# Float32 products of the compression as three float32r products, and a 0/1 operand loaded one chunk earlier

## The chip, the cores and the metric

The kernel runs on one core of a Trainium2 chip. The metric is the device time of one execution in microseconds (us); lower is better. Times of the kernel before are three executions and one profiled execution.

## The reference, cut to what matters

One inference step of a decoder trunk with two layers, for a prompt of 512 positions and eight samples of 8 positions with a past of 1024. Each layer projects its input into columns for a convolution, for sparse attention with three branches and for differential attention. One of the three branches attends to compressed keys and values, and the change lies in this compression:

```python
def nsa_compress(k, pe, w1, b1, w2):
    B, L, G, D = k.shape
    n16 = L // CMP_STRIDE
    k16 = k[:, :n16 * CMP_STRIDE].reshape(B, n16, CMP_STRIDE, G, D)
    blk = jnp.concatenate([k16[:, :-1], k16[:, 1:]], axis=2) + pe[None, None, :, None, :]
    blk = blk.transpose(0, 1, 3, 2, 4).reshape(B, n16 - 1, G, CMP_LEN * D)
    return jax.nn.gelu(blk @ w1 + b1) @ w2
```

CMP_STRIDE is 16, CMP_LEN 32, G 2 and D 64: each block of 32 positions (2048 numbers of a group) is multiplied by w1 (2048 x 128), once for keys and once for values, in both layers. The past of the samples lies in pages that a page table names. The samples' three branches are mixed by sigmoid gates, `o = gate0 * o_cmp + gate1 * o_sel + gate2 * o_win`.

## The kernel before, in words

Each layer first runs two streams of work side by side: `projections()` (the input projection in column chunks b, the convolution's columns, then d, c, q, e, with the convolution's 62 taps on VectorE beside them) and `compressions()` (keys, then values). Both are Python generators that yield the estimated cost of what they have just issued; `merge` always continues the stream that is behind by its share, WP and WC. The tile framework then orders each engine's instructions by a simulated timeline of its own, so an engine's order need not be the program's.

Working tiles come from two sets of SBUF slots: U, 30 slots of 1152 words a partition, and H, 26 slots of 512. `W` takes the slot that has been free longest, and the first write into it waits until the last user is done. `load` issues on SP's queue, in order. `gather` issues an indirect DMA from GpSimd (POOL).

`compress` works in five chunks: four with two samples each (N = 256 columns of output: 2 samples, 2 groups, 64 blocks) and one with the prompt (N = 64). `cmp_keys` gathers a sample's past as 128 partitions (a stretch of 8 positions each, 128 numbers a position), transposes it on TensorE in pieces of 128x128 (L757, eight a tile), and copies each pair out of PSUM with `cp` (L217, nearly always ScalarE), 64 partitions at a time, eight copies a tile. The result kt holds key columns by stretch; a small tail of four columns carries the position term pe, which the first chunk turns into the bias. Then 16 products (L227, as all products) of a float32 piece of w1 by every second column of kt add up in one PSUM bank:

```python
mm(hid[:, :N + 1], w1[k], kt[jp // 2][:, jp % 2, aa:aa + 2 * N + 1:2], k == 0, k == 15)
```

In a trace a float32 product stands as two MATMUL records with a weight load each; a float32r product stands as one. The rest of the kernel's large products are made of float32r parts already: `split` rounds a number to float32r on ScalarE (L187) and subtracts that on VectorE (L190), and three products, high by high, high by low and low by high, take the place of one.

`sample_queries` runs before chunk e. Its first step spreads the samples' gates over partitions by four small products with `selp`, a 0/1 matrix of 64 x 512 that it loads itself from the constants; then it transposes the samples' queries (L1068), which VectorE has scaled at L667.

Of the kernel before, what the change touches and what calls it, by code (L numbers as in the profile page):

```python
# [45 lines left out]
YA = 1.0  # L46
RATIO2 = 3
WP = 125.0
WC = 120.0
WPR = 145.0  # L50
WS = 150.0
ALPHA = (2 * DEPTH) ** 0.25
# [83 lines left out]
def kernel(ctx: ExitStack, tc: tile.TileContext, a: dict, o: dict, nlayers: int = DEPTH):  # L136
# [33 lines left out]
    def T(tag, shape, dt=F):  # L170
        return sb.tile(shape, dt, tag=tag, name=f"{tag}_{next(uid)}", bufs=1)
# [5 lines left out]
    def PS(tag, dt=F):  # L177
        return ps.tile([128, 512], dt, tag=tag, name=f"{tag}_{next(uid)}", bufs=PBUFS[tag])

    def load(out, in_):  # L180
        nc.sync.dma_start(out, in_)
# [31 lines left out]
    def cp(out, in_):  # L213

        if next(turn) % ratio[0] == 1:
            return V.tensor_copy(out, in_)  # L216
        return S.activation(out, in_, AF.Copy)  # L217
# [237 lines left out]
    def layer(l, x, x_src, raws):  # L455
# [165 lines left out]
        def new_kv(br):  # L621
            vv[br] = W("H", [128, 4, 128])
            kH[br], kL[br] = (W("U", [128, 2, SEQ], FR) for _ in range(2))
# [66 lines left out]
        def attention_columns():  # L690
            for c in ORDER:
                if c == "c":
                    new_kv("win")
                if c == "e":
                    sample_queries()
                    yield 2.0
                    own["QK"] = yield from diff_operands(0, "t1")
                yield from chunk(*dict(d=(1816, 512, sink_d), e=(2328, 256, sink_e), c=(1536, 280, sink_c), q=(512, 512, sink_q))[c])
            free(*x[0], *x[1], *x[2])
# [18 lines left out]
        G.memset(vblk, 0.0)  # L718

        def cmp_weights(which):  # L720
            w1s = [W("U", [128, 8, 128]) for _ in range(2)]
            for i in range(2):
                load(w1s[i], a["cmp_w1_" + which][l, i * 1024:(i + 1) * 1024].rearrange("(k p) n -> p k n", p=128))
            w1 = [w1s[k // 8][:, k % 8] for k in range(16)]
            w2p = T("c2", [128, 192])
            G.memset(w2p, 0.0)
            load(w2p[:, 0:64], a["cmp_w2_" + which][l])
            load(w2p[:, 128:192], a["cmp_w2_" + which][l])
            pe = W("H", [16, 128])
            load(pe, a["cmp_pe_" + which][l].rearrange("(k r) d -> k (r d)", r=2))  # L730
            b1 = T("cb" + which, [128, 1])
            load(b1, a["cmp_b1_" + which][l].unsqueeze(1))
            pt = PS("t1")
            PE.transpose(pt[:, :16], pe, ident[:16, :16])
            peT = T("cpe" + which, [128, 2, 2, 4])
            V.tensor_copy(peT, pt[:, :16].rearrange("p (a q i) -> p q i a", q=2, i=2))
            free(pe)
            return w1s, w1, w2p, b1, peT

        def cmp_keys(which, peT, p):  # L740


            n = 128 if p < 4 else 64
            slots = 4 if p < 4 else 2
            kt = [W("U", [128, 2, slots * n + 4]) for _ in range(2)]
            for q in range(2):
                V.tensor_copy(kt[q][:, :, slots * n:], peT[:, q])
            for b2 in range(2 if p < 4 else 1):
                if p < 4:
                    nat = gather("cache_nsa_cmp_" + which, l, 2 * p + b2)  # L750
                else:
                    nat = W("U", [64, 8, 128])
                    load(nat, o["p_cmp_" + which][l, 0].rearrange("(p j) g d -> p j (g d)", j=8))
                for q in range(2):
                    pt = PS("t1").rearrange("p (k t) -> p k t", k=4)
                    for j in range(4):
                        PE.transpose(pt[:, j, :n], nat[:, 4 * q + j], ident[:n, :n])  # L757
                    for g in range(2):
                        c0 = (b2 * 2 + g) * n
                        for par in range(2):  # L760
                            cp(kt[q][par * 64:(par + 1) * 64, :, c0:c0 + n], pt[g * 64:(g + 1) * 64, par::2, :n])
                    yield 0.5
                free(nat)
            return kt

        def cmp_out(which, w2p, p, N, xb):
# [27 lines left out]
        def compress(which):  # L794
            w1s, w1, w2p, bias, peT = cmp_weights(which)
            yield 6.0
            held = None
            for p in range(5):
                kt = yield from cmp_keys(which, peT, p)
                N = 256 if p < 4 else 64  # L800
                hid = PS("h")
                for k in range(16):
                    aa, jp = k // 4, k % 4
                    mm(hid[:, :N + 1], w1[k], kt[jp // 2][:, jp % 2, aa:aa + 2 * N + 1:2], k == 0, k == 15)
                    if k % 4 == 3:
                        yield 1.8
                free(*kt)
                if p == 0:
                    add(bias, hid[:, N:N + 1], bias)
                xb = W("H", [128, N])  # L810
                act(xb, hid[:, :N], AF.Identity, bias=bias)
                t1 = W("H", [128, N])
                act(t1, xb, AF.Square, scale=math.sqrt(0.044715 * GELU_C))
                V.scalar_tensor_tensor(out=t1, in0=t1, scalar=GELU_C, in1=xb, op0=OP.add, op1=OP.mult)
                act(t1, t1, AF.Tanh)
                V.scalar_tensor_tensor(out=xb, in0=t1, scalar=1.0, in1=xb, op0=OP.add, op1=OP.mult)
                free(t1)
                if held:
                    cmp_out(which, w2p, *held)
                held = (p, N, xb)  # L820
                yield 1.5
            cmp_out(which, w2p, *held)
            free(*w1s)

        def compressions():
            yield from compress("k")
# [219 lines left out]
        def sample_queries():  # L1046
            nonlocal QSR, QDs, QS, QR, QD
            QSR, QDs = W("U", [128, 2, 4, 128]), W("U", [128, 2, 4, 128])
            QS, QR = QSR[:, 0], QSR[:, 1]
            QD = [QDs[:, 0], QDs[:, 1]]  # L1050
            qr_s, za_s, zr_s = own["qr"], own["za"], own["zr"]
            pg = PS("t1")
            selp = W("H", [64, 512])
            so = CST["selp"][0]
            load(selp, a["cst"][:64, so:so + 512])
            for p in range(4):
                mm(pg[:, p * 24:(p + 1) * 24], selp[:, p * 128:(p + 1) * 128], gates[:64, 4], True, True)
            free(selp)
            gm = T("gm", [128, 4, 3, 8])
            for p in range(4):  # L1060
                mul(gm[:, p], pg[:, p * 24:(p + 1) * 24].rearrange("p (h r) -> p r h", r=3), C("headm").unsqueeze(1).to_broadcast([128, 3, 8]))
            V.tensor_reduce(grow.rearrange("p a b -> p (a b)"), gm.rearrange("p a b h -> p (a b) h"), axis=AX.X, op=OP.add)
            G.memset(QS, 0.0)
            G.memset(QR, 0.0)
            for src, dst in ((qr_s.rearrange("p (h d) -> p h d", h=4), QS), (za_s.rearrange("p h g d -> p h (g d)"), QR)):
                pt = PS("t1")
                for k in range(4):
                    PE.transpose(pt[:, k * 64:(k + 1) * 64], src[:, k], ident[:64, :64])  # L1068
                for b2 in range(2):
                    for g in range(2):  # L1070
                        gr = slice(g * 64, (g + 1) * 64)
                        c0 = b2 * 64 + g * 32
                        cp(dst[gr, :, c0:c0 + 32].rearrange("p q (k t) -> p q k t", k=4),
                           pt[gr, :256].rearrange("p (k q b t) -> p q b k t", k=4, q=4, b=2)[:, :, b2])
            pt = PS("t1")
            V.tensor_scalar(zr_s[:, :256], zr_s[:, :256], DSCALE, None, op0=OP.mult)
            for k in range(4):
                PE.transpose(pt[:, k * 64:(k + 1) * 64], zr_s[:, k * 128:(k + 1) * 128], ident[:64, :64])
            dm = C("dmask").rearrange("p (f k) -> p f k", f=2)
            for ft in range(2):  # L1080
                for b2 in range(2):
                    src = pt[:, ft * 64:(ft + 1) * 64].rearrange("p (q b t) -> p q b t", q=4, b=2)[:, :, b2]
                    mul(QD[ft][:, :, b2 * 64:(b2 + 1) * 64].rearrange("p q (k t) -> p q k t", k=8), src.unsqueeze(2).to_broadcast([128, 4, 8, 8]),
                        dm[:, ft].unsqueeze(1).unsqueeze(3).to_broadcast([128, 4, 8, 8]))
            cp(ktd.rearrange("p f t -> p (f t)"), pt[:, 128:256])
            free(qr_s, za_s, zr_s)
# [548 lines left out]
```

## Time and profile before

| | |
|---|---|
| median of three executions | 2062.5 us (2058.97 to 2068.48) |
| the profiled execution | 2071.4 us, of which its span (first to last instruction) is 2069.6 |
| TensorE products busy | 1933.5 us (93%), 12222 records |
| TensorE weight loads busy | 1631.7 us (79%) |
| VectorE busy | 1101.2 us (53%) |
| ScalarE busy | 916.7 us (44%) |
| POOL busy | 206.7 us (10%) |
| mean granted TensorE clock | 0.969 of full speed |

All times in the trace are us from the span's start. Busy time of TensorE's products counts each from its start to the modelled end of its drain, so products that follow each other closely overlap, and the pace is read from one start to the next, not from the mean duration. DVE is VectorE, ACT ScalarE, PE TensorE, SP the queue that most loads go through.

### The profile page before, as it was taken

The numbers are of one execution on the slowest core, as the hardware profiler recorded it, in microseconds if no ns is written. First come the engines' busy times: TensorE is split into PE (matmuls) and PEld (weight loads), VectorE is DVE, ScalarE is ACT, GpSimd is POOL, SyncE is SP. The second block draws the span as 40 slices with busy tenths as digits, with TensorE's granted clock in tenths as the row PEclk, the third lists the DMA queues.
The fourth block names the chain that finished last, engine by engine and source line by source line (L and its number), as shares of the span: only waits on it lengthen the run. The fifth ranks groups of instructions, "written<-read, shape, count | busy, mean of one in ns | idle before, by whom it ended". The sixth has DMA issues, their size and how long they took to land. (4 is left out here: it accounts for less than half of the span.)

```text
span 2069.6 us, 32882 instructions
## 1 busy us (share of the span) xinstructions
PE 1933.5 (93%) x12222; PEld 1631.7 (79%) x12222; DVE 1101.2 (53%) x3012; ACT 916.7 (44%) x2368; POOL 206.7 (10%) x233
## 2 busy tenths in 40 slices
PE   8999888989999999999999997989899999999997
PEld 6887765656689999988879776656566899999885
DVE  3568476866573333323456665678666633333236
ACT  3635565767422333321245545667673223333211
POOL 2011022121010000000120110221110000000002
PEclk9999899999999999999999998999999999999999
DMA  6423143243423332352153321441433332324411
GB/s 200 137 76 103 28 145 128 83 146 99 136 92 117 97 122 83 93 187 77 48 174 108 96 71 45 152 155 57 138 108 118 112 122 82 122 84 130 149 56 51
DMA packets 190252, 223.91 MB, mean 108 GB/s; under 512 B 19092, under 2 KB 138812, under 8 KB 189948
## 3 DMA queue, kind: packets, MB, share of 16 engines
q1 hardware_dynamic: 171660, 154.69, 24.5%
q0 software_dynamic: 18432, 67.12, 10.2%
q8 instruction: 97, 1.59, 0.3%
q14 instruction: 63, 0.52, 0.1%
HBM read 206.23 MB, written 24.15 MB: 111 GB/s over the span
## 5 line engine op out<-in xcount | busy, mean ns | idle before, releaser
L227 PE MATMUL a<-H,U 128*128 128x512 f32 (+3 forms) x2264 | 552.8, 411 | 14.0 <-ACT H L187 11.6
L190 DVE TENSOR_TENSOR H<-H,H 128x512 fp32r<-128x512 f32 (+5 forms) x392 | 255.5, 657 | 510.5 <-ACT H L187 482.8
L227 PEld LDWEIGHTS a<-H,U 128*128 128x128 f32 (+1 forms) x2264 | 386.2, 190 | 111.2 <-issue 15.4
L187 ACT ACTIVATE H<-H 128x512 fp32r<-128x512 f32 (+4 forms) x418 | 240.8, 583 | 519.9 <-DMA H<-in_ffn_w_dram 298.8
L227 PE MATMUL a<-U,H 128*128 128x288 f32 (+2 forms) x3008 | 399.2, 306 | 7.9 <-DMA U<-in_cache_diff_v_dram,idx 6.7
L227 PEld LDWEIGHTS a<-U,H 128*128 128x128 f32 (+1 forms) x3008 | 370.2, 181 | 21.7 <-DMA U<-in_cache_diff_v_dram,idx 7.3
L227 PE MATMUL t<-U,H 128*128 128x288 f32 x1584 | 288.7, 297 | 0.4 <-ACT U L187 0.4
L227 PEld LDWEIGHTS t<-U,H 128*128 128x128 f32 x1584 | 243.5, 190 | 1.0 <-ACT U L187 0.6
L227 PE MATMUL a<-U,U 128*128 128x512 f32 (+4 forms) x744 | 200.7, 379 | 7.9 <-ACT H L187 3.7
L227 PE MATMUL h<-U,U 128*128 128x257 f32 (+5 forms) x708 | 152.4, 376 | 13.1 <-ACT U L217 13.0
L217 ACT ACTIVATE U<-t 64x256 f32<-64x256 f32 (+4 forms) x393 | 142.8, 366 | 45.6 <-PE t L757 24.5
L227 PEld LDWEIGHTS a<-U,U 128*128 128x128 f32 x744 | 129.4, 191 | 34.2 <-ACT U L187 7.4
L227 PEld LDWEIGHTS h<-U,U 128*128 128x128 f32 (+1 forms) x708 | 114.6, 185 | 40.3 <-ACT U L217 17.3
L227 PE MATMUL h<-U,H 128*128 128x288 f32 x528 | 140.9, 296 | 0.0
L187 ACT ACTIVATE U<-H 128x288 fp32r<-128x288 f32 (+4 forms) x160 | 64.4, 438 | 143.8 <-DVE H L190 104.1
L217 ACT ACTIVATE H<-t 128x512 f32<-128x512 f32 (+1 forms) x172 | 94.9, 564 | 45.6 <-PE t L1145 23.5
L547 DVE SCALAR_TENSOR_TENSOR U<-U,cw,U 128x512 f32<-128x512 f32 x240 | 109.4, 510 | 0.1
L227 PEld LDWEIGHTS h<-U,H 128*128 128x128 f32 x528 | 99.3, 188 | 0.0
L190 POOL TENSOR_TENSOR U<-U,U 128x512 f32<-128x512 f32 x24 | 33.6, 1417 | 599.1 <-DVE rs_u L321 459.9
L187 ACT ACTIVATE U<-t 128x256 fp32r<-128x256 f32 (+4 forms) x132 | 47.1, 370 | 97.0 <-PE t L350 40.8
L190 DVE TENSOR_TENSOR U<-H,U 128x64 fp32r<-128x64 f32 (+6 forms) x204 | 69.9, 385 | 31.1 <-ACT U L187 24.8
L216 DVE COPY H<-t 128x512 f32<-128x512 f32 (+1 forms) x92 | 57.2, 626 | 45.7 <-PE t L1214 15.6
(293 smaller groups left out, 2268.9 us busy)
## 6 DMA issues: line engine op xcount, KB each, us to landing
H<-in_ffn_w_dram SPq DMA_DIRECT2D x264, 256.0 KB
H<-in_w_in_dram SPq DMA_DIRECT2D x64, 256.0 KB
H<-in_w_out_dram SPq DMA_DIRECT2D x32, 256.0 KB
xd<-U SPq DMA_DIRECT2D x24, 256.0 KB
U<-xd SPq DMA_DIRECT2D x12, 512.0 KB
U<-in_x_prompt_dram SPq DMA_DIRECT2D x8, 512.0 KB
H<-in_state_nsa_win_v_dram SPq DMA_DIRECT2D x16, 256.0 KB
H<-in_state_nsa_win_k_dram SPq DMA_DIRECT2D x16, 256.0 KB
```

The costliest lines, as they stand in the source:

```text
L187: S.activation(out, in_, func, **kw)
L190: return (eng or V).tensor_tensor(out, x, y, op=op)
L216: return V.tensor_copy(out, in_)
L217: return S.activation(out, in_, AF.Copy)
L227: return PE.matmul(out, lhsT, rhs, start=start, stop=stop)
L547: V.scalar_tensor_tensor(out=ac, in0=ex, scalar=wc, in1=ac, op0=OP.mult, op1=OP.add)
```

## The change

The gathered tile is first copied inside SBUF by ScalarE, four copies a tile, into two halves (H slots) whose columns are ordered so that each 128 of them, transposed, are already two positions of one group. The halves are transposed, four pieces each, and `split` into two float32r tiles kt (high and low). w1 is loaded into a passing tile and split into high and low parts, four tiles that are held instead of two. The products of a chunk run in two halves (q), each with its own kt; each float32 product becomes three float32r products. The tail of pe has six columns in two parts, copied by GpSimd instead of VectorE. The cost yields change from 1.8 per four products to 1.4 per twelve, and WC from 120 to 128. `selp` is loaded before chunk q, into an H slot that it holds through that chunk, instead of in `sample_queries`.

```diff
-WC = 120.0
+WC = 128.0
@@ attention_columns
+                if c == "q":
+                    own["selp"] = W("H", [64, 512])
+                    load(own["selp"], a["cst"][:64, CST["selp"][0]:CST["selp"][0] + 512])
@@ cmp_weights
-            w1s = [W("U", [128, 8, 128]) for _ in range(2)]
+            w1s = [[], []]
             for i in range(2):
-                load(w1s[i], a["cmp_w1_" + which][l, i * 1024:(i + 1) * 1024].rearrange("(k p) n -> p k n", p=128))
-            w1 = [w1s[k // 8][:, k % 8] for k in range(16)]
+                raw = W("U", [128, 8, 128])
+                load(raw, a["cmp_w1_" + which][l, i * 1024:(i + 1) * 1024].rearrange("(k p) n -> p k n", p=128))
+                wh, wl = (W("U", [128, 8, 128], FR) for _ in range(2))
+                split(wh, wl, raw)
+                free(raw)
+                w1s[0].append(wh)
+                w1s[1].append(wl)
+            w1 = [(w1s[0][k // 8][:, k % 8], w1s[1][k // 8][:, k % 8]) for k in range(16)]
...
-            peT = T("cpe" + which, [128, 2, 2, 4])
-            V.tensor_copy(peT, pt[:, :16].rearrange("p (a q i) -> p q i a", q=2, i=2))
+            peT = T("cpe" + which, [128, 2, 2, 2, 6], FR)
+            G.memset(peT.bitcast(F), 0.0)
+            split(peT[:, 0, :, :, :4], peT[:, 1, :, :, :4], pt[:, :16].rearrange("p (a q i) -> p q i a", q=2, i=2))
@@ cmp_keys
+        def cmp_keys(nats, q, n, peT):
+            w = 2 * n
+            kt = [W("U", [128, 2, len(nats) * w + 6], FR) for _ in range(2)]
+            for part in range(2):
+                G.tensor_copy(kt[part][:, :, len(nats) * w:], peT[:, part, q].bitcast(F))
+            for b2, nat in enumerate(nats):
+                pt = PS("t1")
+                for i in range(4):
+                    PE.transpose(pt[:, i * n:(i + 1) * n], nat[q][:, i * 128:(i + 1) * 128], ident[:n, :n])
+                split(*(t[:, :, b2 * w:(b2 + 1) * w] for t in kt), pt[:, :2 * w].rearrange("p (i c) -> p i c", i=2))
+                yield 0.5
             return kt
@@ compress
+                    halves = [W("H", [n, 2, 2, 2, 64]) for _ in range(2)]
+                    for q in range(2):
+                        for g in range(2):
+                            act(halves[q][:, :, g], nat[:, 4 * q:4 * q + 4, g * 64:(g + 1) * 64].rearrange("p (i k) d -> p i k d", k=2))
...
+                M = N + 2 if p == 0 else N
                 hid = PS("h")
-                for k in range(16):
-                    aa, jp = k // 4, k % 4
-                    mm(hid[:, :N + 1], w1[k], kt[jp // 2][:, jp % 2, aa:aa + 2 * N + 1:2], k == 0, k == 15)
-                    if k % 4 == 3:
-                        yield 1.8
-                free(*kt)
+                for q in range(2):
+                    kt = yield from cmp_keys(nats, q, 128 if p < 4 else 64, peT)
+                    free(*(t[q] for t in own_))
+                    for aa in range(4):
+                        for i in range(2):
+                            wh, wl = w1[aa * 4 + q * 2 + i]
+                            kh, kl = (t[:, i, aa:aa + 2 * M - 1:2] for t in kt)
+                            first, last = q == aa == i == 0, q == 1 and aa == 3 and i == 1
+                            mm(hid[:, :M], wh, kh, first, False)
+                            mm(hid[:, :M], wh, kl, False, False)
+                            mm(hid[:, :M], wl, kh, False, last)
+                        if aa % 2:
+                            yield 1.4
+                    free(*kt)
@@ sample_queries
-            selp = W("H", [64, 512])
-            so = CST["selp"][0]
-            load(selp, a["cst"][:64, so:so + 512])
+            selp = own.pop("selp")
```

## Rows read from the trace of the kernel before

**Rows 1.** Busy us by stage: PE, PEld, DVE, ACT, POOL; then clock, DMA share, GB/s

```profile
27.00:90.00 63.00, 60.82 (x333) 52.02 (x332) 23.91 (x75) 36.52 (x98) 7.42 (x12) 0.97 0.42 120
90.00:150.00 60.00, 59.97 (x347) 51.80 (x346) 41.81 (x106) 26.89 (x72) 6.42 (x6) 1.00 0.28 83
150.00:200.00 50.00, 46.59 (x274) 40.19 (x272) 45.91 (x136) 27.57 (x77) 10.06 (x6) 1.00 0.35 94
200.00:240.00 40.00, 36.57 (x198) 29.52 (x197) 13.79 (x33) 19.79 (x52) 4.12 (x8) 1.00 0.15 47
240.00:285.00 45.00, 34.31 (x212) 30.99 (x212) 24.74 (x70) 23.82 (x66) 6.70 (x9) 0.73 0.32 89
```

**Rows 2.** PE's groups, shapes apart, 27 to 240 us (busy, mean ns | idle before)

```profile
L227 PE MATMUL h<-U,U 128*128 128x257 f32 x256 | 63.9, 398 | 4.9 <-ACT U L217 4.8
...
L227 PE MATMUL h<-U,U 128*128 128x65 f32 x64 | 7.6, 270 | 0.0
```

**Rows 3.** PE's waits (total us, times, longest), 27 to 240, then 1055 to 1263

```profile
PE h L227 <- ACT U L217: 4.8, 3, 2.2
PE t L757 <- ACT U L217: 2.6, 3, 1.2
PE t L757 <- DMA U<-in_cache_nsa_cmp_v_dram,idx: 1.0, 1, 1.0
...
PE h L227 <- ACT U L217: 5.2, 5, 1.5
PE t L757 <- ACT U L217: 3.6, 4, 1.7
```

**Rows 4.** PE's timeline in a key chunk: start, us, records

```profile
44.68 6.52 PE L227 MATMUL h<-U,U 128*128 128x257 f32 x28
51.05 0.93 PE L757 MATMUL t<-first,U 128*128 128x128 f32 x7
```

**Rows 5.** PE's timeline in projection e, float32r products of 256 columns

```profile
279.62 0.52 PE L227 MATMUL a<-H,U 128*128 128x256 f32 x3
279.97 0.52 PE L227 MATMUL a<-U,U 128*128 128x256 f32 x3
280.33 0.52 PE L227 MATMUL a<-H,U 128*128 128x256 f32 x3
```

**Rows 6.** PE's timeline, the small chunk of the values

```profile
222.80 3.46 PE L227 MATMUL h<-U,U 128*128 128x65 f32 x30
```

**Rows 7.** PE's timeline, float32r products of 128 columns

```profile
389.81 0.42 PE L227 MATMUL a<-U,U 128*128 128x128 f32 x2
390.07 0.23 PE L227 MATMUL a<-causal_b,ident_b 128*128 128x128 bf16 x1
```

**Rows 8.** ACT's and DVE's groups, shapes apart, 20 to 258 us

```profile
L217 ACT ACTIVATE U<-t 64x256 f32<-64x256 f32 x127 | 48.1, 379 | 13.3 <-PE t L757 11.6
L187 ACT ACTIVATE H<-H 128x512 fp32r<-128x512 f32 x25 | 15.4, 629 | 12.3 <-DMA H<-in_w_in_dram 7.9 <-PE t L502 3.3 <-DVE H L816 0.5
L187 ACT ACTIVATE H<-H 128x256 f32<-128x256 f32 x16 | 6.6, 415 | 2.4 <-DVE H L814 2.2
...
L190 DVE TENSOR_TENSOR H<-H,H 128x512 fp32r<-128x512 f32 x25 | 17.2, 691 | 12.6 <-ACT H L187 12.0
...
L658 DVE SCALAR_TENSOR_TENSOR U<-t,U 64x512 fp32r<-64x512 f32 x4 | 2.8, 688 | 1.6 <-ACT U L187 1.5
```

**Rows 9.** DMA issues: count and median us from issue to landing

```profile
U<-in_cache_nsa_cmp_k_dram,idx POOLq DMA_INDIRECT x16, 5.2
```

**Rows 10.** Timelines of SP, PE and DVE around the gates' products

```profile
242.52 0.53 SPq L181 DMA_DIRECT2D H<-in_cst_dram  x1
...
245.12 1.90 PE L227 MATMUL t<-gates,H 64*128 64x24 f32 x8 [4.55 <-DMA H<-in_cst_dram]
246.85 0.66 PE L1068 MATMUL t<-first,H 64*128 64x64 f32 x4
...
244.59 0.41 DVE L667 TENSOR_SCALAR H<-H 64x512 f32<-64x512 f32 x1
```

More of the change, by code (lines that the diff above doesn't have):

```diff
@@ L734, in cmp_weights @@
             PE.transpose(pt[:, :16], pe, ident[:16, :16])
-            peT = T("cpe" + which, [128, 2, 2, 4])
-            V.tensor_copy(peT, pt[:, :16].rearrange("p (a q i) -> p q i a", q=2, i=2))
+            peT = T("cpe" + which, [128, 2, 2, 2, 6], FR)
+            G.memset(peT.bitcast(F), 0.0)
+            split(peT[:, 0, :, :, :4], peT[:, 1, :, :, :4], pt[:, :16].rearrange("p (a q i) -> p q i a", q=2, i=2))
             free(pe)
             return w1s, w1, w2p, b1, peT
[L740 to L763, printed above, removed]
+        def cmp_keys(nats, q, n, peT):
[9 more added lines that the diff above has]
+                yield 0.5
             return kt
@@ L798, in compress @@
             for p in range(5):
-                kt = yield from cmp_keys(which, peT, p)
+                nats, own_ = [], []
+                for b2 in range(2 if p < 4 else 1):
+                    if p < 4:
+                        nat, n = gather("cache_nsa_cmp_" + which, l, 2 * p + b2), 128
+                    else:
+                        nat, n = W("U", [64, 8, 128]), 64
+                        load(nat, o["p_cmp_" + which][l, 0].rearrange("(p j) g d -> p j (g d)", j=8))
+                    halves = [W("H", [n, 2, 2, 2, 64]) for _ in range(2)]
+                    for q in range(2):
+                        for g in range(2):
+                            act(halves[q][:, :, g], nat[:, 4 * q:4 * q + 4, g * 64:(g + 1) * 64].rearrange("p (i k) d -> p i k d", k=2))
+                    nats.append([t.rearrange("p i g k d -> p (i g k d)") for t in halves])
+                    own_.append(halves)
+                    free(nat)
+                    yield 0.5
                 N = 256 if p < 4 else 64
+                M = N + 2 if p == 0 else N
                 hid = PS("h")
-                for k in range(16):
-                    aa, jp = k // 4, k % 4
-                    mm(hid[:, :N + 1], w1[k], kt[jp // 2][:, jp % 2, aa:aa + 2 * N + 1:2], k == 0, k == 15)
-                    if k % 4 == 3:
-                        yield 1.8
-                free(*kt)
+                for q in range(2):
[12 more added lines that the diff above has]
+                    free(*kt)
                 if p == 0:
@@ L822, in compress @@
             cmp_out(which, w2p, *held)
-            free(*w1s)
+            free(*w1s[0], *w1s[1])
         def compressions():
```

## The prediction

> **What bounds the kernel now.** The first view is the table by stage [rows 1]: one layer's projections and compressions run together from 27 to 240 us (the other layer repeats it from 1055 to 1263). TensorE is shown busy for 204 of those 213 us, at a granted clock of 0.97 to 1.00, that is the 2.4 GHz level. VectorE has 125 of 213 us, but 45.9 of the 50 between 150 and 200; ScalarE 111 of 213. So this stage is bound by TensorE's queue of products, with VectorE close behind in one stretch. After 240 us the picture changes: TensorE 34.3 of 45 us at a mean clock of 0.73, so partly at 1.2 GHz. There it waits for others.
>
> The second view is TensorE's groups in that stage [rows 2]. A compression's first product in float32 appears as two MATMUL records, so 256 records are 128 products (4 chunks of 16, for k and v), and 128 per layer make 256 in both layers; 64 records of 65 columns are the fifth, smaller chunk.
>
> The third is the list of TensorE's waits [rows 3]. In the compression work it waits 4.8 + 5.2 us before the products (until ScalarE has copied the transposed keys out of PSUM) and 2.6 + 1.0 + 3.6 us before transposes. The stage is nearly full, so a microsecond less of TensorE work there is nearly a microsecond of span, as long as its operands come in time.
>
> **The first products.** In the timeline, 28 records of 257 columns start at 44.68 and the next form starts at 51.05 [rows 4]; the same rows, less one record's drain, give (6.52 - 0.39) / 27 = 0.227 us a record, and from start to start 6.37 / 28 = 0.2275. So a product takes 0.455 us. Three products on split float32r operands, with 256 moving columns, stand in the trace too: in the last projection each group of three starts 0.35 to 0.36 us after the group before it [rows 5], so 0.355 us, weight loads included. Gain: 256 x (0.455 - 0.355) = 25.6 us.
>
> The small chunk goes the other way. Its 32 records now cost (3.46 - 0.27) / 29 = 0.110 us each [rows 6], where 65 columns at the long record's pace would give 0.058, so a pace per record sets it and not the columns. It gets 48 products. At the same 0.110 that is 5.3 us for 3.5; no float32r product of 64 columns is in the trace, the nearest (128 columns) are 0.13 us apart [rows 7], which gives 6.2 us. Four such chunks cost 4 x 1.8 = 7.0 us, at most 4 x 2.7 = 11. I take 7, since that pace should hold for records with weights of the same width. Transposes keep their number and size. TensorE's work falls by 25.6 - 7.0 = 18.6 us.
>
> The new moving operand takes every second column, as the old one did. No row shows a float32r operand read so. At one extreme it streams as the contiguous one; at the other it falls to the rate of the float32 records, 0.2275 us each, which is the rival priced below. I take the first: the float32r rows have the same type and width, the float32 rows only the same step.
>
> The Trainium skill (SBUF — State Buffer, Door 1: The DMA port swizzle) says that SBUF is read in lines of 16 bytes, that full bandwidth wants at least two hits a line, and that each crossing to a new line costs. A step of two float32 elements gives exactly two hits, so by that rule the gain above stands; no run here shows it yet. Another page (FP8 and Floating Point Precision, TensorE Precision Notes) counts true float32 as four passes; three for four would make 0.341 us of 0.455 and a gain of 29 us, where the rows give 0.355.
>
> **What feeds them.** Before, each gathered tile was transposed as it came, and eight ScalarE copies of 64x256 took it out of PSUM, 379 ns each, 3.0 us [rows 8]. Now four copies of 128x256 inside SBUF come first (415 ns each by the nearest row), and after the transposes two splits of 128x512: ScalarE 629 and VectorE 688 ns each. So ScalarE has 2.9 us instead of 3.0, and VectorE 1.4 us more, a tile. The weights are split too: four tiles of 128x1024 a layer. By the 512 column rows (629 and 691) I estimate twice each less an overhead, 1.1 us of ScalarE and 1.2 of VectorE. Per layer: ScalarE about +2 us. VectorE 16 x 1.4 + 5 + 2 (prompt tiles) - 3 (the small tail copies, now on POOL) = +26 us, to 151 of some 204 us. On average this is hidden behind TensorE's 200 us. It is not hidden wherever VectorE is at 9 tenths [rows 1]; there, some 50 us a layer, the low halves queue behind the convolution's taps.
>
> The pipeline is also cut finer. A chunk's products were one batch of 16 behind its transposes; now there are two batches of 24, each with transposes and a split ahead of it. The ends of 40 half chunks replace those of 20. If each half chunk start waits as a chunk start does now, the 10.0 us of waits before the products [rows 3] become 20.0: +10. Waits before transposes I hold equal: they waited for a PSUM bank, and now also for a ScalarE copy that waits for the gather. Bounds: 0 (the projections' products fill in between, and a split is two steps where four copies stood) and, with every chain exposed, more than the whole gain (below).
>
> The gathers land 5.2 us after their issue [rows 9]. The four held weight tiles are two more of the 30 large slots, so a gather's slot comes free later; and what waits for a late gather is now ScalarE's queue, with the projections' weight splits behind it, not TensorE alone. I put nothing on it: only 1.0 us of wait for a gather shows in the first layer.
>
> On POOL: the tail copies and one memset, some 42 a layer, in a queue that is mostly idle; what stands behind them are the gathers. Nothing.
>
> The pacing constant 120 to 128 and lower costs let the compressions end earlier beside the projections; the products of both are the same, so no term of its own.
>
> **The gates' operand.** TensorE idles 4.55 us until 245.12 for this load; the load was issued only at 242.52, when its slot came free [rows 10]. Loaded a chunk ahead, past eight weight loads on SP's queue (128 KB more ahead of them, which are ahead of need), it ends that wait. Late next are the transposes at 246.85: they need the queries that VectorE scales at 244.59 for 0.41 us, so 245.0. The 1.9 us of gate products slip into the gap, and the transposes start 1.8 us earlier. I take 1.8 x 2 = 3.6 us; bounds 0 (the next projection's weights, whose loads wait for slots, are the real limit) and 2 x 4.55 = 9.1.
>
> **Sum.** -25.6 + 7.0 + 10 - 3.6 = -12.2 us. The profiled execution took 2071.4 us, 2069.6 of it span; it would take 2059. The median before, 2062.5, lies 9 below that execution, so I forecast 2062.5 - 12.2 = 2050. Below 0.5%, 10 us, a measurement of this kernel can hardly tell from no change (its three runs spread by 9.5).
>
> **Rivals.**
> *The gain is swallowed.* VectorE, at 46 of 50 us, gets some 11 us more for the v chunks (8 tiles x 1.4) in that neighbourhood. If 4 to 7 us of it a layer hold up TensorE on top of the 10, the result is -4 to +2: 2058 to 2064. For it speaks the table by stage; against it, VectorE is 34% busy right after, from 200 to 240.
>
> *The half chunk starts decide* (slower). A chain of four copies (1.7), transposes (0.6), a ScalarE split (0.6) and a VectorE split (0.7) is 3.6 us long, 40 times. If 1.2 us of it is exposed each time, 48 us come instead of 10: 2050 + 38 = 2088. From 22.2 / 40 = 0.56 us each nothing is gained. Against it: other products are interleaved at every step now, and the k chunks of the first layer show almost no wait.
>
> *The strided operand streams at half rate* (slower). As a mechanism here: the operand's step halves the columns a float32r product takes in per us, three products at 0.2275 take 0.6825 for 0.455 us, 256 x 0.2275 = +58, and with +7 and -3.6 the kernel takes 2124. For it: no row shows such a read. Against it: nothing but the pace of the float32 rows, which would have to be set by their passes alone. The Trainium skill (SBUF — State Buffer, Door 1: The DMA port swizzle) lets a step of two float32 pass just at its limit.
>
> *Only the load helps*, the float32r products gaining nothing net: 2059; its chance is in that of the swallowed gain.
>
> **Chances.** The forecast (2038 to 2056) 0.52; swallowed 0.27; half chunk starts 0.13; half rate 0.06; 0.02 for better. The range runs from the small stall bound and the larger load gain, 2062.5 - 24, to some way into the half chunk case: 2038 to 2076. Faster by over 0.5% 0.53, within 0.27, slower 0.20.
>
> **What would show it.** Right: 768 records of 256 or 258 columns 0.115 to 0.12 us apart; small products 0.11; TensorE's stage from 27 to 240 shorter by 6 to 10 us in each layer; the wait for the constant gone and one for VectorE or ScalarE, 2 to 3 us, in its place. Wrong: spacing of 0.2 and more; new waits of TensorE for VectorE's low halves or for ScalarE's splits beyond 15 us in both layers; ScalarE idle for gathers; a longer stretch at 1.2 GHz.

## The result, and the profile after

The changed kernel takes 2158.9 us (median of four, 2157.7 to 2164.1) where the kernel before takes 2065.5: a ratio of 1.0445, with a 95% interval from 1.0415 to 1.0474. That is 92 us slower, outside the range that was given. The profiled execution spans 2155.9 us.

TensorE's groups of the compression's first products, over the whole span (busy us, mean ns, then idle time ahead of them):

```profile
L227 PE MATMUL h<-U,U 128*128 128x256 f32 x576 | 143.1, 414 | 8.8 <-ACT H L187 4.4 <-DVE U L190 2.9 <-ACT U L187 1.4
...
L227 PE MATMUL h<-U,U 128*128 128x258 f32 x192 | 46.9, 416 | 0.0
...
L227 PE MATMUL h<-U,U 128*128 128x64 f32 x192 | 27.6, 308 | 1.4 <-ACT U L187 0.9 <-DVE U L190 0.5
```

Three groups hold 217.6 us of busy time, where one layer's two groups before held 63.9 + 7.6 [rows 2], so about 143 in both. The work that was to shrink by 19 us grew by some 75. TensorE's timeline in the two halves of the keys' second chunk (start, us, records) shows why:

```profile
60.31 5.44 PE L227 MATMUL h<-U,U 128*128 128x256 f32 x23
...
67.85 5.52 PE L227 MATMUL h<-U,U 128*128 128x256 f32 x23 [0.25 <-DVE U L190]
```

23 records take 5.44 us; less the last one's 0.39, that is 5.05 / 22 = 0.230 us each, the pace of a float32 record with its 257 columns [rows 4], and not the 0.118 of the float32r rows [rows 5]. Three of them take 0.69 us where one product took 0.455.

Around the gates' products the wait for the constant is gone, and TensorE now waits for a ScalarE split (of the next projection's weights) instead:

```profile
282.96 1.07 PE L227 MATMUL t<-gates,H 64*128 64x24 f32 x8
...
288.61 1.02 PE L227 MATMUL a<-H,U 128*128 128x256 f32 x4 [3.99 <-ACT H L187]
```

The splits cost what was expected. ScalarE's and VectorE's groups from 20 to 290 us:

```profile
L187 ACT ACTIVATE H<-U 128x256 f32<-128x256 f32 x56 | 19.2, 405 | 12.8 <-DMA U<-in_cache_nsa_cmp_v_dram,idx 9.7 <-DMA U<-in_cache_nsa_cmp_k_dram,idx 2.2 <-DVE U L190 0.4
L187 ACT ACTIVATE U<-t 128x512 fp32r<-128x512 f32 x32 | 18.8, 596 | 44.2 <-PE t L760 38.8 <-DVE U L190 2.9 <-POOL U L756 2.4
L187 ACT ACTIVATE U<-U 128x1024 fp32r<-128x1024 f32 x4 | 4.2, 1050 | 0.0
...
L190 DVE TENSOR_TENSOR U<-t,U 128x512 fp32r<-128x512 f32 x32 | 21.9, 688 | 24.5 <-ACT U L187 24.3
```

New beside them: ScalarE stood idle 9.7 + 2.2 us ahead of its permuting copies, waiting for gathers.

### The profile page after: what moved, and what is told of

It reads as the page before. It is cut to its first block, busy times and chain, and to the rows that moved or that the text cites. A ratio compares the mean times of both kernels' runs of the same rounds, so it can differ in the third digit from the quotient of the medians.

```text
span 2155.9 us, 33651 instructions
## 1 busy us (share of the span) xinstructions
PE 2011.0 (93%) x12542; PEld 1712.5 (79%) x12542; DVE 1149.1 (53%) x3049; ACT 905.0 (42%) x2311; POOL 217.9 (10%) x317
## 4 chain that ended last, share of the span: by engine, by line
PE 62%; DVE 7%; ACT 4%; DMA 3%; issue 1%; POOL 0%; DVEq 0%; ACTq 0%; POOLq 0%; SPq 0%
PE a L227 36%; PE h L227 11%; PE t L227 11%; ACT U L187 2%; PE t L1166 1%; DVE U L190 1%; ACT H L187 1%; PE t L1008 1%; DMA H<-in_w_out_dram 1%; DVE H L190 1%; ACT H L217 1%; DVE pnm L993 1%; DMA U<-in_cache_diff_k_dram,idx 1%; PE t L1235 0%; PE t L760 0%
## 5 line engine op out<-in xcount | busy, mean ns | idle before, releaser
L227 PE MATMUL a<-H,U 128*128 128x512 f32 (+3 forms) x2264 | 553.8, 412 | 30.6 <-ACT H L187 25.6
L187 ACT ACTIVATE H<-H 128x512 fp32r<-128x512 f32 (+5 forms) x418 | 241.3, 583 | 511.9 <-DMA H<-in_ffn_w_dram 299.2
L227 PE MATMUL h<-U,U 128*128 128x256 f32 (+4 forms) x1028 | 230.0, 400 | 13.1 <-ACT H L187 4.4
L227 PEld LDWEIGHTS h<-U,U 128*128 128x128 f32 (+1 forms) x1028 | 190.6, 212 | 38.3 <-issue 5.0
L187 ACT ACTIVATE U<-t 128x256 fp32r<-128x256 f32 (+5 forms) x204 | 86.8, 440 | 171.6 <-PE t L760 78.5
L190 DVE TENSOR_TENSOR U<-t,U 128x512 fp32r<-128x512 f32 (+3 forms) x196 | 87.5, 455 | 90.5 <-ACT U L187 60.4
```

The source lines that it names most:

```text
L187: S.activation(out, in_, func, **kw)
L190: return (eng or V).tensor_tensor(out, x, y, op=op)
L227: return PE.matmul(out, lhsT, rhs, start=start, stop=stop)
```

## The experiments

All are compared with runs of the kernel before on the same chip. Its medians lie between 2065.5 and 2071.5 us from chip to chip, so ratios are what counts.

### The step of two

**Even and odd key columns in separate halves.** The split writes the transposed keys so that each product reads neighbours. The tail of pe follows the same order; that part is left out here. Nothing else is changed.

```diff
-            kt = [W("U", [128, 2, len(nats) * w + 6], FR) for _ in range(2)]
+            kt = [W("U", [128, 2, 2, len(nats) * n + 3], FR) for _ in range(2)]
...
-                split(*(t[:, :, b2 * w:(b2 + 1) * w] for t in kt), pt[:, :2 * w].rearrange("p (i c) -> p i c", i=2))
+                split(*(t[:, :, :, b2 * n:(b2 + 1) * n] for t in kt), pt[:, :2 * w].rearrange("p (i c r) -> p i r c", i=2, r=2))
...
-                            kh, kl = (t[:, i, aa:aa + 2 * M - 1:2] for t in kt)
+                            kh, kl = (t[:, i, aa % 2, aa // 2:aa // 2 + M] for t in kt)
```

> The changed kernel, but the split writes even and odd key columns into separate halves of kt, so that each float32r product reads 256 neighbouring columns; same numbers of instructions, same result. Theory (the step of two halves the pace of a float32r product): records of 256 columns go from 0.228 to about 0.118 us, 768 x 0.11 = 84 us less, so 2159 - 84 = 2075, a little above the kernel before. Rival (the pace comes from something else in these products, such as three weight loads for one bank, or the tiles' place): records stay at 0.228 and the time at 2159. Rival (VectorE and ScalarE pay for reading PSUM with a step): the records get faster, but the splits get longer than 0.69 us and the time falls by less.

Measured: 2095.5 us, ratio 1.0144 (1.0112 to 1.0176). Of the 92 us, 63 are gone, where the expectation had 84. TensorE's timeline:

```profile
57.34 2.89 PE L227 MATMUL h<-U,U 128*128 128x256 f32 x23
```

(2.89 - 0.28) / 22 = 0.119 us a record, as expected. The groups over the whole span say where part of the other 21 us stayed:

```profile
L227 PE MATMUL h<-U,U 128*128 128x256 f32 x576 | 89.4, 309 | 13.4 <-DVE U L190 6.3 <-ACT H L187 3.8 <-ACT U L187 3.3
...
L227 PE MATMUL h<-U,U 128*128 128x258 f32 x192 | 25.7, 284 | 0.0
```

The large groups fall from 143.1 + 46.9 to 89.4 + 25.7 us, by 75, and the waits before them rise from 8.8 to 13.4. The splits are no longer for it, although they now read PSUM with a step (VectorE and ScalarE, 20 to 290 us):

```profile
L190 DVE TENSOR_TENSOR U<-t,U 128x512 fp32r<-128x512 f32 x32 | 21.9, 686 | 13.1 <-ACT U L187 13.0
...
L187 ACT ACTIVATE U<-t 128x512 fp32r<-128x512 f32 x32 | 18.8, 596 | 30.8 <-PE t L762 20.1 <-POOL U L758 5.3 <-DVE U L190 5.2
```

**Neighbouring columns, nothing else.** The layout stays; the products read other columns, so other numbers are multiplied.

```diff
-                            kh, kl = (t[:, i, aa:aa + 2 * M - 1:2] for t in kt)
+                            kh, kl = (t[:, i, aa:aa + M] for t in kt)
```

> The changed kernel with nothing changed but the moving operand of the compression's first products: neighbouring columns instead of every second one (other numbers are multiplied). Theory: 0.118 us a record, about 2075, and what is still above the kernel before, some 10 us, is the price of the rest of the change. Rival: no change, 2159.

Measured: ratio 1.0187 (1.0152 to 1.0222), 2101.7 us, with the same pace:

```profile
46.03 2.91 PE L227 MATMUL h<-U,U 128*128 128x258 f32 x23
```

It is the read, not the layout. Half of the slices in these two kernels start at an odd element, and the mean pace is still 0.119, so the start does not matter.

**Every fourth column** (again other numbers).

```diff
-                            kh, kl = (t[:, i, aa:aa + 2 * M - 1:2] for t in kt)
+                            kh, kl = (t.rearrange("p i c -> p (i c)")[:, aa:aa + 4 * M - 3:4] for t in kt)
```

> The changed kernel, moving operand of the first products reads every fourth column (other numbers are multiplied). If each float32r read takes two neighbouring elements and a step of two wastes one, a step of four wastes no more: 0.228 us a record and 2159. If the pace falls with the bytes passed over, or with 16 byte lines touched (one use a line instead of two), records take about 0.44 us and the kernel some 2159 + 768 x 0.21 = 2320.

Measured once: 2164.5 us. The timeline:

```profile
61.50 5.53 PE L227 MATMUL h<-U,U 128*128 128x256 f32 x23
```

(5.53 - 0.39) / 22 = 0.234 us. A step of four costs what a step of two does. So what is paid is not bytes passed over, nor lines touched. That float32r elements are fetched in pairs of neighbours, and any step uses one of each pair, fits all three runs; it is argued from them, not shown by itself.

**The float32 products with neighbouring columns**, in the kernel before (other numbers).

```diff
-                    mm(hid[:, :N + 1], w1[k], kt[jp // 2][:, jp % 2, aa:aa + 2 * N + 1:2], k == 0, k == 15)
+                    mm(hid[:, :N + 1], w1[k], kt[jp // 2][:, jp % 2, aa:aa + N + 1], k == 0, k == 15)
```

> The kernel before with the float32 products of the compression reading neighbouring columns (other numbers are multiplied). Theory (a float32 record is paced by its passes, the step of two costs it nothing): 0.227 us a record as before, same time. Rival (it too pays for the step): 0.12 us a record and some 50 us less.

Measured once: 2066.3 us. The timeline, to be held against [rows 4]:

```profile
43.18 6.23 PE L227 MATMUL h<-U,U 128*128 128x257 f32 x28
49.25 0.93 PE L757 MATMUL t<-first,U 128*128 128x128 f32 x7
```

6.07 / 28 = 0.217 us instead of 0.2275. So float32 pays 0.010 us for the step, float32r 0.111. The old product's easy pace said nothing of how the new one would read.

The changed kernel's own trace adds what this pace does not depend on. One of its later batches, and then the stage rows of the batch at 60.31 and of most of this one (the granted clock is the third number from the end):

```profile
185.75 5.75 PE L227 MATMUL h<-U,U 128*128 128x256 f32 x24 [2.21 <-ACT H L187]
```

```profile
60.00:66.00 6.00, 6.00 (x30) 5.37 (x29) 1.42 (x6) 2.53 (x8) 1.29 (x5) 1.00 0.51 154
186.50:189.90 3.40, 3.40 (x16) 3.39 (x15) 3.40 (x11) 2.53 (x8) 2.23 (x1) 0.50 0.18 36
```

For 3.4 of its 5.75 us this batch had the 1.2 GHz level, and still took (5.75 - 0.39) / 23 = 0.233 us a record, against 0.230 at 2.4 GHz. Records with neighbouring columns do follow the clock: 0.119 us at 2.4 GHz and 0.224 at 1.2 (further down, under the clock). So with a step of two, 256 columns take about 0.23 us at either level, and the step costs float32r much at 2.4 GHz and next to nothing at 1.2. The float32 record with a step, 0.2275, stands near the same figure; that one limit of the read holds both is argued, not shown.

### The gates' operand

**The early load alone**, on the kernel before.

```diff
+                if c == "q":
+                    own["selp"] = W("H", [64, 512])
+                    load(own["selp"], a["cst"][:64, CST["selp"][0]:CST["selp"][0] + 512])
...
-            selp = W("H", [64, 512])
-            load(selp, a["cst"][:64, so:so + 512])
+            selp = own.pop("selp")
```

> The kernel before with only the gates' 0/1 operand loaded a chunk ahead. By the prediction's step: the wait of 4.55 us at the gates' products falls to about 2.5 in each layer, 3.6 us less, 2062 instead of 2065.5. Rival: hidden, because the next projection's weights set the time there, 0.

Measured: ratio 1.0049 (1.0032 to 1.0066), 10 us slower. TensorE's timeline in the first layer, to be held against [rows 10]:

```profile
246.85 1.07 PE L227 MATMUL t<-gates,H 64*128 64x24 f32 x8
248.34 0.46 PE L1069 MATMUL t<-first,H 64*128 64x64 f32 x4 [0.42 <-ACT H L187]
250.11 0.43 PE L1069 MATMUL t<-first,H 64*128 64x64 f32 x4 [1.32 <-ACT U L217]
251.81 0.69 PE L1079 MATMUL t<-first,H 64*128 64x64 f32 x4 [1.27 <-ACT U L217]
254.89 1.12 PE L649 MATMUL t<-first,H 128*128 128x128 f32 x4 [2.39 <-DVE U L658]
```

The 4.55 us of wait are gone and 5.4 us of others stand in their place, one behind the other: the chain through ScalarE's and VectorE's copies of the queries was as late as the constant. Before, the gates' products began at 245.12, behind a wait; now they begin at 246.85, behind none. Where the rest of the 10 us comes from (one small slot less during projection q, another order of the instructions) was not taken apart.

**Even and odd columns apart, with the load late again.** Of the first experiment, only the load is put back.

> Even and odd columns in separate halves as in the first experiment, and the gates' operand loaded where the kernel before loads it. Theory (the early load alone costs about 10 us, as it did on the kernel before): 2095 - 10 = 2085. Rival (its cost there was a chance of the order in which instructions fall, not the load): anything from 2085 to 2105.

Measured: ratio 1.0072 (1.0049 to 1.0096), so 0.7% less than with the early load. The early load costs in both kernels. This is the base of the next runs: 0.7% above the kernel before, 15 us, and by the prediction's sum it has 18.6 us less of TensorE's work. The traces show less. The groups of these products over the whole span, in the kernel before and then here:

```profile
L227 PE MATMUL h<-U,U 128*128 128x257 f32 x512 | 126.5, 395 | 10.2 <-ACT U L217 10.1
...
L227 PE MATMUL h<-U,U 128*128 128x65 f32 x128 | 15.2, 270 | 0.0
```

```profile
L227 PE MATMUL h<-U,U 128*128 128x256 f32 x576 | 88.1, 307 | 17.2 <-ACT U L187 8.0 <-DVE U L190 5.2 <-ACT H L187 3.8
...
L227 PE MATMUL h<-U,U 128*128 128x258 f32 x192 | 25.9, 285 | 0.0
...
L227 PE MATMUL h<-U,U 128*128 128x64 f32 x192 | 22.8, 279 | 0.0
```

Busy time falls from 141.7 to 136.8 us, by 5, and the waits before the products rise by 7. Part of the missing gain is records that ran at the 1.2 GHz level (see the clock, below); part may be only apparent, since twice as many batches count twice as many drains.

### What takes the rest

**The permuting copies on POOL instead of ScalarE.**

```diff
-                            act(halves[q][:, :, g], nat[:, 4 * q:4 * q + 4, g * 64:(g + 1) * 64].rearrange("p (i k) d -> p i k d", k=2))
+                            G.tensor_copy(halves[q][:, :, g], nat[:, 4 * q:4 * q + 4, g * 64:(g + 1) * 64].rearrange("p (i k) d -> p i k d", k=2))
```

> As the one before, with the four copies that permute a gathered tile moved from ScalarE to POOL. Theory (ScalarE's queue, held by copies that wait for gathers, makes the projections' weight splits late): the waits of TensorE for those splits, some 24 us in both layers, halve, and the time falls by about 10 us. Rival (the waits come from weights that are loaded late for lack of slots): they stay. Rival (POOL, whose copies of this size take over 0.8 us and which also issues the gathers, becomes late): TensorE waits for it and the time rises.

Measured: ratio 1.0148 (1.0106 to 1.0190), slower. TensorE's waits for the projections' weight splits are not fewer. From 20 to 300 and from 1050 to 1330, with the copies on ScalarE and then here:

```profile
PE a L227 <- ACT H L187: 11.7, 6, 2.7
...
PE a L227 <- ACT H L187: 12.0, 7, 3.0
```

```profile
PE a L227 <- ACT H L187: 12.4, 6, 3.6
...
PE a L227 <- ACT H L187: 13.2, 8, 3.1
```

This speaks against ScalarE's copies, as a queue that holds up the weights, being the cause. It does not exclude them: POOL, which issues the gathers, got 128 copies of 518 ns each (62 us) here, and what that cost was not taken apart.

**Slots held in the kernel before**, unused, through each compression.

```diff
+            held_slots = [W("U", [128, 1024]) for _ in range(2)] + [W("H", [128, 512]) for _ in range(4)]
...
-            free(*w1s)
+            free(*w1s, *held_slots)
```

> The kernel before, with two more of the large and four of the small slots held, unused, through each compression, about what the changed kernel holds for split weights and permuted halves. Theory (fewer slots make loads and gathers late): 10 us or more above the kernel before. Rival (slots are not what is short): within 5 us of it.

Measured: ratio 1.0060 (1.0035 to 1.0085), 12 us. No instruction was added. ScalarE's waits for projection weights still in flight, from 27 to 245 in the kernel before and to 255 in this one and in the one with columns apart:

```profile
ACT H L187 <- DMA H<-in_w_in_dram: 7.9, 6, 3.2
```

```profile
ACT H L187 <- DMA H<-in_w_in_dram: 25.9, 15, 3.8
```

```profile
ACT H L187 <- DMA H<-in_w_in_dram: 20.2, 13, 4.0
```

With fewer slots ScalarE more often finds weights not yet there: 7.9, 25.9 and 20.2 us. But in the kernel before this does not reach TensorE. Its waits from 20 to 300, first in the kernel before, then with slots held:

```profile
PE a L227 <- ACT H L187: 3.7, 3, 2.5
```

```profile
PE t L649 <- DVE U L658: 5.2, 1, 5.2
...
PE a L227 <- ACT H L187: 2.5, 4, 1.4
```

Its wait for weight splits did not grow; a wait for VectorE's low halves of the queries (L658) stands there instead. With columns apart it is the wait for weight splits that grew, to 11.7 us. So what held slots cost this kernel is shown; that the version with columns apart loses its time by the same path is not.

**A faster pace in the kernel before**, 120 to 136.

> The kernel before with the compressions' share raised from 120 to 136, so that they end at the same fraction of the projections as in the changed kernel. Theory (the early end takes filler work from the last projections, where TensorE waits): 5 to 10 us above the kernel before. Rival: no difference.

Measured: ratio 1.0035 (1.0015 to 1.0055), 7 us; a loss, as expected.

**A slower pace with columns apart**, 128 to 112, the counterpart.

> Even and odd columns apart, gates' operand late, and the compressions' share 112 instead of 128, so that they end at about the fraction of the projections at which they ended in the kernel before. Theory (the early end costs what the faster pace cost the kernel before, some 7 us): from 0.7% to about 0.4% above the kernel before. Rival (it is the slots and the feeding): still 0.7%.

Measured: ratio 1.0131 (1.0104 to 1.0157), worse than at 128. So the early end is not what the changed kernel pays for. That its slots, held longer, cost more than the filler brings is a guess that no run tests. What the faster pace cost the kernel before did not carry over to this one.

**One batch a chunk.** The keys of both halves first, then 48 products.

```diff
+                kts = []
                 for q in range(2):
-                    kt = yield from cmp_keys(nats, q, 128 if p < 4 else 64, peT)
+                    kts.append((yield from cmp_keys(nats, q, 128 if p < 4 else 64, peT)))
                     free(*(t[q] for t in own_))
+                for q in range(2):
+                    kt = kts[q]
```

> Even and odd columns apart, operand late, share 128, but a chunk's keys are transposed and split for both halves before its products begin, so that one batch of 48 products follows, not two of 24. Theory of the prediction (each half chunk start waits, 20 more waits): TensorE's waits before these products halve and the time falls by 5 to 10 us from 0.7% above. Rival (two more large tiles are held, slots are what is short): no gain, or slower.

Measured: ratio 1.0060 (1.0041 to 1.0080), against 1.0072 (1.0049 to 1.0096): no gain beyond the intervals. The waits before the large group's products did fall, from 17.2 us to 4.6 (whole span):

```profile
L227 PE MATMUL h<-U,U 128*128 128x256 f32 x576 | 83.8, 301 | 4.6 <-ACT H L187 4.2 <-ACT U L187 0.3
```

So these waits can be taken away without a shorter kernel. This version also holds two more large tiles a chunk, the rival of its expectation, and the two are not told apart.

**One convolution tap of 31**, in the kernel before and in the one with columns apart, which leaves out nearly all of the convolution.

```diff
-                for w in range(CW):
+                for w in range(1):
```

> The kernel before with one convolution tap of 31 computed, which takes some 60 us a layer off VectorE's queue. A base for the next run. Since TensorE bounds that stage, it should be only a little faster than the kernel before, 0 to 15 us.

> The kernel with even and odd columns apart and the load late, with one convolution tap of 31. Theory that VectorE's fullness takes the gain: without the taps it is 10 to 18 us faster than the one before with one tap. Rival (slots, pace, ScalarE's queue and the clock take it): it stays 5 to 15 us slower than that.

Measured: 0.9960 (0.9941 to 0.9978) and 1.0010 (0.9996 to 1.0023) of the kernel before. The second is 1.0010 / 0.9960 = 1.005 times the first. With VectorE emptied of some 60 us a layer the loss goes from 0.7% to 0.5%. The expected 10 to 18 us below the first did not come, so VectorE's fullness is not what takes the gain; whether it is a part of the loss lies within the intervals.

**The keys alone** as float32r products with columns apart; values as before, load late, share 116.

> Three float32r products, with even and odd columns in separate halves, for the compressed keys alone; the values as in the kernel before, the gates' operand loaded late, the compressions' share 116, so that they end at the same fraction of the projections as before. Theory (what the fast products gain is lost to the values' stretch, where slots are few and VectorE is near full, and to the earlier end): about half of the 18.6 us of TensorE work is gained without that loss, 5 to 9 us below the kernel before. Rival (feeding the split operands costs as much in the keys' stretch): at or above the kernel before.

Measured: ratio 1.0007 (0.9991 to 1.0022), no change. **And in one batch a chunk:**

> The keys alone as three float32r products, share 116, with one batch of 48 products a chunk. Theory (half chunk starts): 3 to 6 us below the version with two batches, so a little below the kernel before. Rival: the same as that, within 0.2% of the kernel before.

Measured: ratio 1.0022 (1.0006 to 1.0037). Neither beats the kernel before. The keys-alone trace shows one place where time is handed back. Its timeline at the values' fourth chunk (its products are still float32):

```profile
207.50 0.33 PE L606 MATMUL t<-first,H 128*128 128x128 f32 x1 [1.83 <-DVE U L190]
...
211.93 2.08 PE L227 MATMUL h<-U,U 128*128 128x257 f32 x4 [1.03 <-ACT U L217]
...
214.99 6.16 PE L227 MATMUL h<-U,U 128*128 128x257 f32 x20
```

After waits of 1.83 and 1.03 us the float32 records run (6.16 - 0.39) / 19 = 0.30 us apart on average, at 0.2275 before: part of them ran at the 1.2 GHz level (the stage from 200 to 240 has a mean clock of 0.87, before 1.00 [rows 1]).

## Why the prediction was wrong

**The step that failed** is the choice of a pace for the new moving operand: "I take the first: the float32r rows have the same type and width, the float32 rows only the same step." Both ends were on the page, 0.118 and 0.2275; the records came at 0.230. The step of two sets the pace of a float32r product, and the nearest row in type was not the nearest in what counted. So the sum's first term, -25.6 us, came out as 256 x (3 x 0.230 - 0.455) = +60. The rival named for it (half rate) was the case, with a chance of 0.06, and its 58 us for this term were right. Its 2124 was still 35 us short of what was measured. Of these, 14 are the gates' operand and 5 the small chunk (both below), 2 the pace and 3 the base (2065.5 for 2062.5); the other 11 were not taken apart. Taking the step away brought 63 us and not the 84 that the paces give, so the pace is the main cause and not all of the loss.

The prediction weighed the Trainium skill's rule on this point (SBUF — State Buffer, Door 1: The DMA port swizzle), by which two hits in a line of 16 bytes suffice. The runs disagree for a float32r moving operand: 0.230 us at a step of two, 0.234 at four, 0.119 for neighbours. The measurement decides.

**The gates' operand**, -3.6 us, came out as +10 (0.49%, and 0.7% between the two kernels with columns apart). The step named the transposes as late next, from 245.0, but priced only VectorE's scaling. It missed the chain of copies behind them, on which TensorE now waits 5.4 us. Why the whole costs 10 us and not nothing was not taken apart.

**The half chunk starts**, +10 us. TensorE's waits before those products were 8.8 + 1.4 us in the changed kernel, as much as before; but its records took twice the forecast time, which may leave more time for the next operand. At the forecast pace, with columns apart and the load late, they were 17.2 us, not far from the 20 of the forecast. That they decide the time is not borne out: in one batch they were 4.6 and the time was the same within the intervals.

**The small chunk**, +7: its 192 records take 27.6 us of busy time against 15.2 before, which is +12 and past the upper bound of 11. The pace that was taken, 0.110, was right all the same; what was missing is the clock. The keys' small chunk of the first layer, with columns apart and the load late, and then in the changed kernel:

```profile
118.82 5.44 PE L227 MATMUL h<-U,U 128*128 128x64 f32 x48
```

```profile
135.17 7.06 PE L227 MATMUL h<-U,U 128*128 128x64 f32 x48
```

The first had a granted clock of 1.00: (5.44 - 0.27) / 47 = 0.110 us. The second had 0.75 on the mean, so half of its time at 1.2 GHz. The first version's 192 records hold 22.8 us, which is +7.6.

**What feeds them** was priced well, instruction by instruction (405, 596, 688, 1050 and 1238 ns for 415, 629, 688, 1100 and 1200), but "I put nothing on it" for the slots was wrong. With the step and the early load taken away the kernel is still 0.7% slower. Held slots alone cost the kernel before 0.6%, though by other waits of TensorE. The rival of the swallowed gain named VectorE's fullness; with VectorE emptied the gain did not come back. The gathers that were put at nothing show up as 9.7 + 2.2 us in which ScalarE stood idle.

**The clock.** Table by stage of the version with columns apart and the load late, one row a layer:

```profile
27.00:240.00 213.00, 194.84 (x1255) 175.46 (x1254) 142.43 (x356) 98.43 (x257) 47.14 (x71) 0.93 0.32 95
1055.00:1263.00 208.00, 187.81 (x1223) 168.96 (x1221) 144.71 (x361) 97.27 (x256) 46.34 (x72) 0.93 0.34 100
```

A mean of 0.93 of full speed is (1 - 0.93) x 2 x 213 = 30 us at the 1.2 GHz level, where the kernel before has at most 4 [rows 1: 0.97 over 63 us]. Later stretches give some of it back: over the whole span the mean is 0.961 here and 0.969 before, or 163 and 128 us at the 1.2 GHz level. Its timeline shows what went before:

```profile
162.53 3.11 PE L227 MATMUL h<-U,U 128*128 128x256 f32 x24 [1.90 <-ACT H L187]
165.48 0.60 PE L759 MATMUL t<-first,H 128*128 128x128 f32 x4
168.10 0.38 PE L227 MATMUL h<-U,U 128*128 128x256 f32 x1 [2.02 <-DVE U L190]
...
170.31 1.12 PE L759 MATMUL t<-first,H 128*128 128x128 f32 x4 [1.15 <-ACT H L187]
171.07 4.19 PE L227 MATMUL h<-U,U 128*128 128x256 f32 x18
```

Two waits of 2 us, and then 18 records (4.19 - 0.38) / 17 = 0.224 us apart instead of 0.12, at a granted clock of 0.50: the same products at half the clock. So short waits here can cost twice, once for themselves and once for the slower products behind them. Not each one does: after the 1.90 us at 162.53 the 24 records still run (3.11 - 0.28) / 23 = 0.123 us apart. At half speed for 35 us more than before, some 17 us of work are lost over the whole kernel if TensorE bounds all of them, an upper estimate from these means. The prediction's sum counted waits once.

**What stays open.** How the last 0.7% divides among slots, waits and the clock was not settled. The direct test, more slots for the version with columns apart, was not made. No version that was run beats the kernel before.

## What to carry to other kernels

Before a float32 product is replaced by float32r ones, look at how its moving operand is read: with neighbouring columns three products cost 0.36 us here where one cost 0.455, with a step of two or four 0.69 and 0.70 (all at 2.4 GHz). Let the step be taken where it is free, in the copy that writes the operand (a split from PSUM took 596 and 688 ns with and without). And where a stage is full on TensorE and its slots rotate, price held slots as you price instructions: two large and four small ones cost this kernel 12 us without a single operation. Where an experiment takes a cause away, compare what comes back with what the paces promise, and look for the rest in the trace: here 63 us came of 84.

## What the runs showed of the hardware that was not expected

At 2.4 GHz a float32r product of 256 columns runs at 0.119 us with neighbouring columns, 0.230 with every second and 0.234 with every fourth; whether it starts at an even or an odd element does not matter. At 1.2 GHz neighbouring columns take 0.224 us, and every second column still 0.23: the limit of the stepped read does not follow TensorE's clock. A float32 record of 257 columns runs at 0.217 and 0.2275, so it hides nearly all of the same step. ScalarE and VectorE read PSUM with a step of two at the speed of neighbours.
